# A two-block transformer step on one core: products with tokens on the partitions

## The chip, the cores and the metric

The kernel runs on one core of a Trainium2 chip. A core has a matrix engine (TensorE, "PE" in the profile, with its weight loads as "PEld"), VectorE ("DVE"), ScalarE ("ACT"), GpSimd ("POOL") and SyncE ("SP"), 16 DMA engines, an on-chip memory of 128 partitions (SBUF) and the accumulator banks that PE writes (PSUM). The metric is the device time of one execution, in microseconds (us); lower is better.

## The reference

A sequence of 256 tokens with 1024 features goes through two blocks, all in float32:

```python
def first_block(x, ...):
    h = rms_norm(x, norm1_g)
    y_a = rwkv(h @ w_in[...])             # 8 heads, recurrence with decay
    y_b = sparse_attention(h @ w_in[...]) # 8 heads, top-k keys by an indexer
    ga, gb = sigmoid(h @ w_in[...gates])
    x = x + (ga * (y_a @ w_o_rwkv) + gb * (y_b @ w_o_att)) @ w_out
    h = rms_norm(x, norm2_g)
    x = x + (silu(h @ w_gate) * (h @ w_up)) @ w_ffn_out   # 2816 hidden
    return rms_norm(x, normf_g)

def second_block(x, c, ...):
    sh1, sc1, gt1, sh2, sc2, gt2 = split(silu(c) @ w_ada + b_ada, 6)
    h = rms(x, g_mix) * (1 + sc1) + sh1
    y_a = gated_deltanet(h @ w_in[...])   # conv, chunked delta rule
    y_b = dilated_mixture(h @ w_in[...])  # three window/dilation patterns
    merged = sigmoid(gate_a) * (y_a @ w_up_gdn) + sigmoid(gate_b) * (y_b @ w_up_dil)
    x = x + gt1 * (merged @ w_out)
    h2 = rms(x, g_ffn) * (1 + sc2) + sh2
    return x + gt2 * moe_ffn(h2, ...)     # 64 experts, 8 per token, and a shared one
```

## The kernel before

**How a product is made.** The weights are float32 in DRAM. `wsplit` cuts what a load brought into pieces of 1024 columns and each piece into two matmul-ready parts: ACT casts the high part (`wh`, L269), DVE subtracts it from the weight and writes the rest (`wl`, L270), 512 columns at a time, in a ring of three pieces. Activations are split in the same way (`uh`, `ul`). A product of two such pairs is three matmuls (`mm3`: high by high, high by low, low by high) in the fp32r format.

**How a product lies.** The residual stream `xT` and nearly every activation are feature-major: features on the 128 partitions, the 256 tokens along the free axis, eight blocks side by side. `dense` (L296) holds a 128x128 block of the weights still in PE and moves the 256 tokens past it, so that one PSUM bank takes two blocks of 128 output features. PSUM banks of the tag `d` come in a ring of four. Only the attention values of the two blocks (`vps`, `vdp`) hold the tokens still and move the weights, 256 columns at a time.

**Norms.** `Rms` squares a block (ACT L368), gathers the squares on DVE (L376 to L379) and sums over the partitions by matmuls with ones on PE (`nps`, L386 to L395 turn the sum into 1/rms in each partition). Gains are numbers for a partition.

**The order of work.** Block 1: norm, `w_in` products, RWKV and sparse attention with gate products slipped between their steps (`fill`), then output products: `merge` (L878) multiplies the gate of the attention branch by its output product (DVE L873), adds the other branch (POOL L881), and splits the result into `mgh` (ACT L883) and `mgl` (DVE L884) for the product with `w_out`; the residual sum (DVE L910) and its norm follow. The feed-forward network runs 11 groups of 256 hidden features: the gate and up products of group g+1 stand ahead of the down product of group g, which adds up in four PSUM banks (`acc`, tags `a` and `b`); `gated` (L923) makes the activation between them. During these groups DVE also computes block 2's modulation vector (`ada_step`, 24 steps). Block 2 has the same form: norm and modulation, products, DeltaNet and dilated attention with fills, four rounds of gate product and `merge`, `w_out_2`, norm, router. Then come the experts: 27 half-units that stream 1 MB expert weights, gather the tokens of an expert, run it and scatter its output into four `acc` banks (L1662) by a matmul with a permutation. At the end eight DVE steps (L1759) add `acc` times gt2 to the residual, with an output DMA behind each second step.

PE's instructions run in the order in which the scheduler and, in the expert stage, the code wrote them; an engine that waits holds back all that stands behind it in its own queue.

Of the kernel before, what the change touches and what calls it, by code (L numbers as in the profile page):

```python
# [16 lines left out]
D = 1024  # L17
S = 256
# [118 lines left out]

def lay_out(inp):
# [24 lines left out]
    A["w_in_2"] = wgroups(np.concatenate([w2[:, :4096], w2[:, 4112:]], 1), 256)  # L163
    A["w_ba"] = wgroups(w2[:, 4096:4112], 16)[0]
    A["up_g"] = wgroups(np.asarray(inp["w_up_gdn_2"])[0], 256)
    A["up_d"] = wgroups(np.asarray(inp["w_up_dil_2"])[0], 256)
    A["w_out_2"] = wgroups(np.asarray(inp["w_out_2"])[0], 256)
# [26 lines left out]
def _body(es, tc, A, pat, cat, taps, upto):  # L194
# [111 lines left out]

    def whole(steps):
# [90 lines left out]
    nrm = cp.tile([128, 1], F32, name="nrm")  # L398

# [357 lines left out]
    def dsa_proj():  # L757
# [15 lines left out]
        for i in range(2):  # L773
            rope((yield from dense(A["w_in"][13 + i], uu)), [(every, qi[:, 2 * i:2 * i + 2])])
# [4 lines left out]
        for i in range(2):  # L779
            p = pt("d", "vps")  # L780
            for k, (wh, wl) in enumerate(wblocks(A["w_in"][11 + i], 256)):
                for n in range(2):
                    tk = slice(128 * n, 128 * (n + 1))
                    mm3(p[:, 256 * n:256 * (n + 1)], (uu[0][:, k, tk], uu[1][:, k, tk]), (wh, wl), k == 0 and n == 0, k == NB - 1)
                yield
            nc.scalar.copy(vt[:, :, 256 * i:256 * (i + 1)], p.rearrange("p (n c) -> p n c", n=2))

    ga = ap_.tile([128, NB, S], F32, name="ga", tag="s1", bufs=1)
    gcol = lambda t, g: fl(t[:, 2 * g:2 * g + 2])

    def gate_steps(t, src):

        nc.scalar.activation(t, (yield from dense(src, uu)), AF.Tanh, scale=0.5)
# [5 lines left out]
    for g in range(4):  # L799
        fill.add("ga", gate_steps(gcol(ga, g), A["w_in"][15 + g]))  # L800
# [61 lines left out]
    gb = rp.tile([128, NB, S], F32, name="gb", tag="zr", bufs=2)  # L862
# [25 lines left out]
    for g in range(4):  # L888
        first_term(gcol(ga, g), A["wo_r"][g], ysp, 4)
    for g in range(4):  # L890
        gate_group(gcol(gb, g), g, A["w_in"][19 + g])
    tap("ya", fl(yA))
    tap("yb", fl(yB))
    if upto == 2:
        return
# [3 lines left out]
    for g in range(4):  # L899
        merge(mg, g, gcol(ga, g), gcol(gb, g), A["wo_a"][g], ysp, 4)  # L900
    xT = ap_.tile([128, NB, S], F32, name="hT1", tag="s0", bufs=1)
    norm = Rms(xT, r2(0))
    more_slots(dp, 1, "qq")
    for g in range(4):
# [9 lines left out]
    tap("h1", fl(xT))  # L914
    if upto == 3:
        return
# [6 lines left out]
    def gated(fp, pg, pu, hi, lo):  # L923

        t = fp.tile([128, 512], F32, name="silu", tag="silu")
        nc.scalar.activation(t, pg, AF.Silu)
        nc.vector.tensor_tensor(t, t, pu, op=ALU.mult)
        nc.scalar.copy(hi, t)
        nc.vector.tensor_sub(lo, t, hi.bitcast(F32))

    def accumulate(acc, src, act, first, last):

        order = [(k, ct) for k in range(2) for ct in range(NB)]
        w = iter(wsplit(src))
        if last:
            w, order = list(w), [(k, ct) for ct in range(NB) for k in range(2)]
        parts_ = []
        for k, ct in order:
            if len(parts_) <= k:
                parts_ = list(w) if last else parts_ + [next(w)]  # L940
            wh, wl = parts_[k]
            c = slice(128 * ct, 128 * (ct + 1))
            o = 256 * (ct % 2)
            mm3(acc[ct // 2][:, o:o + 256], (wh[:, c], wl[:, c]), (act[0][:, k, :], act[1][:, k, :]),
                first and k == 0 and ct % 2 == 0, last and k == 1)
# [28 lines left out]
    _, uu, _ = scaled_parts(xT, lambda b: pcol("norm2_g", b), norm.finish())  # L974
    acc = [pt("ab"[i % 2], "acc%d" % i) for i in range(4)]
    steps = iter(range(24))
    gate = lambda g: dense_pair(A["ffn_in"][g], uu)
    acts = []
    pg = gate(0)
    for g in range(11):  # L980
        pu = gate(11 + g)
        acts.append(tuple(fp.tile([128, 2, S], F32R, name="act" + x, bufs=3) for x in "hl"))
        gated(fp, pg, pu, *(fl(x) for x in acts[g]))
        if g < 10:
            pg = gate(g + 1)
# [12 lines left out]
    more_slots(None, 0)
    fx.close()
# [10 lines left out]
    with tc.issue_after(d.ins):  # L1010
        rs1 = norm.finish()
# [802 lines left out]
```

## Time and profile before

| what | us |
|---|---|
| runs of the kernel (three) | 1529.07, 1529.05, 1523.01; median 1529.05 |
| the profiled execution, its own time | 1525.53 |
| its span in the trace | 1523.7 |
| PE busy | 1444.0 |
| DVE busy | 823.8 |
| ACT busy | 586.4 |
| POOL busy | 119.6 |

The span is the time from the first to the last instruction that the profiler saw; about 1.8 us of the execution lie around it. The busy times of the engines overlap. PE's mean granted clock is 0.981 of full speed. The expert stage begins near 1023 us in this trace and lasts for the rest of the span.

### The profile page before, as it was taken

What the parts mean: (1) busy time and instruction counts of PE and PEld (TensorE: products, weight loads), DVE (VectorE), ACT (ScalarE), POOL (GpSimd) and SP (SyncE); (2) the same over time, 40 slices, a digit from 0 to 9 for tenths busy, and PEclk for the clock granted to TensorE, in tenths of its full rate; (3) what the DMA queues carried; (4) which work ended last, traced back from release to release, by engine and by line L of the source; (5) the groups of instructions that cost most, each with busy time, mean ns of one, the idle gap of its engine ahead of it and who ended that gap; (6) DMA issues with size and microseconds to landing.
All of it is one profiled execution on the core that took longest, in us unless ns stands there. A gap on an engine that the chain in (4) does not pass through costs nothing.

```text
span 1523.7 us, 27838 instructions
## 1 busy us (share of the span) xinstructions
PE 1444.0 (95%) x11234; PEld 1162.8 (76%) x11234; DVE 823.8 (54%) x1671; ACT 586.4 (38%) x1200; POOL 119.6 (8%) x120
## 2 busy tenths in 40 slices
PE   6999999989999979899999999989999999989996
PEld 6799998979999969798898999987554544444543
DVE  5787488668888787855855567654122111111211
ACT  5543256545444467444534555442111111111110
POOL 2143210100000000310230000100000000000000
PEclk9999999989999989999999999999999999999999
DMA  6302154649877255222321433983999999999996
GB/s 222 116 31 69 39 172 131 217 177 419 351 290 283 95 191 194 84 83 74 121 84 56 166 115 107 337 325 142 358 405 421 422 421 421 421 422 421 421 421 259
DMA packets 58626, 362.09 MB, mean 238 GB/s; under 512 B 6912, under 2 KB 7552, under 8 KB 20352
## 3 DMA queue, kind: packets, MB, share of 16 engines
q1 hardware_dynamic: 56912, 357.77, 60.6%
q10 hardware_dynamic: 1584, 2.52, 0.5%
q8 instruction: 89, 1.46, 0.4%
q14 instruction: 41, 0.34, 0.1%
HBM read 357.51 MB, written 1.05 MB: 235 GB/s over the span
## 4 chain that ended last, share of the span: by engine, by line
PE 77%; DMA 13%; DVE 6%; ACT 2%; POOL 1%; issue 1%; SPq 0%; DVEq 0%; ACTq 0%; POOLq 0%
PE dps L283 35%; DMA wx<-in_w_exp_dram 9%; PE gup L283 8%; PE acc L283 6%; PE sps L283 5%; PE dnp L283 4%; DMA wh<-in_w_exp_dram 2%; PE gat L283 2%; PE vdp L283 2%; DVE wl L270 1%; PE sps L286 1%; PE sgu L283 1%; DMA wl<-in_w_exp_dram 1%; PE ksp L283 1%; PE vps L283 1%
## 5 line engine op out<-in xcount | busy, mean ns | idle before, releaser
L283 PE MATMUL dps<-uh,wh 128*128 128x256 f32 x1280 | 379.2, 297 | 13.2 <-ACT uh L416 8.9
L283 PE MATMUL dps<-uh,wl 128*128 128x256 f32 x1280 | 369.1, 289 | 2.4 <-DVE wl L270 2.4
L283 PE MATMUL dps<-ul,wh 128*128 128x256 f32 x1280 | 369.6, 289 | 0.1
L283 PEld LDWEIGHTS dps<-uh,wh 128*128 128x128 f32 x1280 | 248.3, 194 | 24.9 <-ACT uh L416 10.3
L283 PEld LDWEIGHTS dps<-ul,wh 128*128 128x128 f32 x1280 | 248.6, 194 | 6.1 <-issue 4.3
L283 PEld LDWEIGHTS dps<-uh,wl 128*128 128x128 f32 x1280 | 248.3, 194 | 4.3 <-DVE wl L270 2.8
L270 DVE TENSOR_TENSOR wl<-w,wh 128x512 fp32r<-128x512 f32 x267 | 193.1, 744 | 68.6 <-ACT wh L269 66.7
L283 PE MATMUL gup<-wx,xg 128*32 128x512 f32 (+2 forms) x1016 | 202.1, 600 | 18.7 <-DMA wx<-in_w_exp_dram 18.6
L269 ACT CAST wh<-w 128x512 fp32r<-128x512 f32 x267 | 154.2, 614 | 147.1 <-PE dps L283 99.9
L269 ACT CAST wh<-wm 128x512 fp32r<-128x512 f32 x200 | 115.7, 618 | 128.5 <-PE dps L283 84.1
L270 DVE TENSOR_TENSOR wl<-wm,wh 128x512 fp32r<-128x512 f32 x200 | 137.7, 718 | 48.8 <-ACT wh L269 48.4
L283 PEld LDWEIGHTS gup<-wx,xg 128*32 128x32 f32 (+2 forms) x1016 | 59.6, 121 | 134.9 <-issue 95.9
L1658 DVE TENSOR_TENSOR yl<-dnp,yh 128x512 fp32r<-128x512 f32 x54 | 37.3, 691 | 156.6 <-ACT yh L1657 156.6
L1632 DVE COPY cs<-pxt 128x1 f32<-128x1 f32 x27 | 4.3, 158 | 213.8 <-PE pxt L286 213.8
L283 PE MATMUL dnp<-wx,hT 128*32 128x512 f32 (+1 forms) x528 | 102.0, 597 | 3.3 <-DMA wx<-in_w_exp_dram 2.5
L1638 ACT ACTIVATE sgx<-gup 128x256 f32<-128x256 f32 x27 | 10.3, 383 | 219.9 <-PE gup L283 219.9
L1657 ACT CAST yh<-dnp 128x512 fp32r<-128x512 f32 x54 | 31.6, 585 | 123.0 <-PE dnp L283 123.0
L283 PEld LDWEIGHTS dnp<-wx,hT 128*32 128x32 f32 (+1 forms) x528 | 27.8, 120 | 48.7 <-issue 39.5
L283 PE MATMUL acc<-PT,yh 128*128 128x256 f32 x216 | 55.2, 293 | 0.0
L283 PE MATMUL gat<-P,hth 128*128 128x256 f32 (+1 forms) x224 | 54.7, 287 | 0.0
L283 PE MATMUL acc<-PT,yl 128*128 128x256 f32 x216 | 53.1, 283 | 0.6 <-DVE yl L1658 0.6
L957 DVE SCALAR_TENSOR_TENSOR ada<-wm,ct,ada 128x512 f32<-128x512 f32 x76 | 53.2, 744 | 0.0
(520 smaller groups left out, 2789.6 us busy)
## 6 DMA issues: line engine op xcount, KB each, us to landing
wx<-in_w_exp_dram SPq DMA_DIRECT2D x159, 1024.0 KB, 16.0
w<-in_w_in_dram SPq DMA_DIRECT2D x44, 1024.0 KB, 4.9
wm<-in_w_ada_dram SPq DMA_DIRECT2D x22, 1024.0 KB, 8.0
wm<-in_w_in_dram SPq DMA_DIRECT2D x21, 1024.0 KB, 4.9
wh<-in_w_exp_dram SPq DMA_DIRECT2D x33, 512.0 KB, 15.9
wl<-in_w_exp_dram SPq DMA_DIRECT2D x33, 512.0 KB, 14.7
wm<-in_ffn_in_dram SPq DMA_DIRECT2D x16, 1024.0 KB, 9.1
wm<-in_ffn_out_dram SPq DMA_DIRECT2D x7, 1024.0 KB, 7.1
```

What stands on the lines that cost most here:

```text
L269: nc.scalar.copy(hi[:, c:e], x[:, c:e])
L270: nc.vector.tensor_sub(lo[:, c:e], x[:, c:e], hi[:, c:e].bitcast(F32))
L283: latest[0] = nc.tensor.matmul(*args, **kw)
L286: latest[0] = nc.tensor.transpose(*args, **kw)
L957: nc.vector.scalar_tensor_tensor(y, x, ct[:, k:k + 1], y, op0=ALU.mult, op1=ALU.add)
L1632: nc.vector.tensor_copy(self.cs, px[:, 256:257])
L1638: nc.scalar.activation(sg, self.pg[:, 0:256], AF.Silu)
L1657: nc.scalar.copy(yh[:, quar(c, 512)], pd)
L1658: nc.vector.tensor_tensor(yl[:, quar(c, 512)], pd, yh[:, quar(c, 512)].bitcast(F32), op=ALU.subtract)
```

## The change

**Products.** `dense_t` replaces `dense` for the values, all gates, all output projections (`wo_r`, `wo_a`, `w_out`, `up_g`, `up_d`, `w_out_2`) and the feed-forward network: a 128x128 block of the activations (128 tokens) stands still in PE and the weights move past it 512 columns wide. It fills two PSUM banks, one for each half of the tokens (n), with 512 output features (c) each; k runs outside, n inside. The products for RWKV's and DeltaNet's inputs, queries, keys and the indexer stay as they were. Weights are laid out for this in DRAM; each load is still 1 MB.

**The residual stream** `xt` is token-major: tokens on the partitions, features along the free axis. `Means` sums the squares along the free axis with ACT's accumulator. Where a product needs the features on the partitions again, `turned` makes four 128x128 PE transposes into a PSUM bank: in `merge`, after both norms of block 1 and block 2's, and twice two transposes in each feed-forward group (`gated`). The vectors gt1 and gt2 are spread over the partitions by eight matmuls each (`gtp`), and the final norm's gain comes as a DRAM array of 128 equal rows (`gfrow`). The scatter holds the permutation still and moves the expert's output 512 wide. At the end DVE multiplies by gt2, and the sum with the residual is DVE's for the first half of the tokens and POOL's for the second.

```diff
+    def dense_t(srcs, u, name="dpt", early=False):
+
+        p = [pt("d", name) for _ in range(2)]
+        srcs = [srcs[i] for i in range(srcs.shape[0])]
+        last = 4 * len(srcs) - 1
+        for i, src in enumerate(srcs):
+            pieces = wsplit(wload(src))
+            for ks in ([range(4)] if early and i == len(srcs) - 1 else [(k,) for k in range(4)]):
+                for n in range(2):
+                    for k4 in ks:
+                        k, o = 4 * i + k4, slice(512 * (k4 % 2), 512 * (k4 % 2) + 512)
+                        wh, wl = pieces[k4 // 2]
+                        mm3(p[n], (u[0][:, k, toks[n]], u[1][:, k, toks[n]]), (wh[:, o], wl[:, o]), k == 0, k == last)
+                        yield
+        return p
+
+    def turned(src, name="trp"):
+
+        p = pt("d", name)
+        for b in range(4):
+            tr(p[:, 128 * b:128 * (b + 1)], src[:, 128 * b:128 * (b + 1)], ident)
+        return p.rearrange("p (b t) -> p b t", b=4)
...
-    def merge(mg, g, t, m, w, y, nk):
-
-        first_term(m, w, y, nk)
-        nc.gpsimd.tensor_tensor(t, t, m, op=ALU.add)
-        hi, lo = (fl(q[:, 2 * g:2 * g + 2]) for q in mg)
-        nc.scalar.activation(hi, t, AF.Copy, scale=0.5)
-        nc.vector.scalar_tensor_tensor(lo, t, 0.5, hi.bitcast(F32), op0=ALU.mult, op1=ALU.subtract)
+    def merge(mg, c, t, m, mc, src, y):
+
+        first_term(m, mc, src, y)
+        for n in range(2):
+            x = t[:, n, c5[c]]
+            nc.gpsimd.tensor_tensor(x, x, m[:, n, c5[mc]], op=ALU.add)
+            p = turned(x)
+            hi, lo = (q[:, 4 * c:4 * c + 4, toks[n]] for q in mg)
+            nc.scalar.activation(hi, p, AF.Copy, scale=0.5)
+            nc.vector.scalar_tensor_tensor(lo, p, 0.5, hi.bitcast(F32), op0=ALU.mult, op1=ALU.subtract)
...
-    for g in range(4):
-        t = r2(1)("xres")
-        nc.scalar.dma_start(out=fl(t), in_=A["xT"][:, 512 * g:512 * (g + 1)])
-        p = dense_pair(A["w_out"][g], mg)
-        if g:
-            norm.pair(g - 1)
-        nc.vector.tensor_tensor(fl(xT[:, 2 * g:2 * g + 2]), p, fl(t), op=ALU.add)
-    norm.pair(3)
+    nc.scalar.activation(nrm, epsd[:, 0:1], AF.Sqrt)
+    for c in range(2):
+        p = whole(dense_t(A["w_out"][c], mg, early=c == 1))
+        for n in range(2):
+            t = fl(r2(1)("xres"))
+            nc.scalar.dma_start(out=t, in_=A["x"][:, D * n + 512 * c:D * n + 512 * (c + 1)])
+            nc.vector.tensor_tensor(xt[:, n, c5[c]], p[n], t, op=ALU.add)
+            means.add(n, 0, c, xt[:, n, c5[c]], nx[:, n, c5[c]])
+    uu = parts()
+
+    def normed2(b, p):
+        g = pcol("norm2_g", b)
+        nc.scalar.activation(uu[0][:, b, toks[n]], p, AF.Copy, scale=g)
+        nc.vector.scalar_tensor_tensor(uu[1][:, b, toks[n]], p, g, uu[0][:, b, toks[n]].bitcast(F32), op0=ALU.mult, op1=ALU.subtract)
+
+    for n in range(2):
+        rs = means.inverse(n)
+        for c in range(2):
+            nc.vector.tensor_scalar(nx[:, n, c5[c]], xt[:, n, c5[c]], rs, None, op0=ALU.mult)
+            p = turned(nx[:, n, c5[c]])
+            for b in range(4):
+                normed2(4 * c + b, p[:, b])
...
+    def gated(p, hi, lo):
+
+        q = pt("d", "act").rearrange("p (b t) -> p b t", b=2)
+        for n in range(2):
+            t = fp.tile([128, 256], F32, name="silu", tag="silu")
+            nc.scalar.activation(t, p[n][:, 0:256], AF.Silu)
+            nc.vector.tensor_tensor(t, t, p[n][:, 256:512], op=ALU.mult)
+            for b in range(2):
+                tr(q[:, b, toks[n]], t[:, 128 * b:128 * (b + 1)], ident)
+        nc.scalar.copy(hi, q)
+        nc.vector.tensor_sub(lo, q, hi.bitcast(F32))
...
+    means = Means(2)
+    for n in range(2):
+        for c in range(2):
+            x, y = xt[:, n, c5[c]], hg[:, n, c5[c]]
+            nc.vector.tensor_tensor(x, acc[n][c], x, op=ALU.add)
+            nc.vector.tensor_tensor(y, x, gfrow[:, c5[c]], op=ALU.mult)
+            for kind, z in enumerate((x, y)):
+                j = fp.tile([128, 512], F32, name="junk", tag="junk", bufs=2)
+                means.add(n, kind, c, z, j)
+        rsb = means.inverse_both(n)
+        for c in range(2):
+            q = fp.tile([128, 512], F32, name="hq", tag="hq", bufs=2)
+            nc.vector.tensor_scalar(q, hg[:, n, c5[c]], rsb, None, op0=ALU.mult)
+            p = turned(q)
+            for b4 in range(4):
+                b = 4 * c + b4
+                hi, lo = (z[:, b, toks[n]] for z in uu)
+                t = fp.tile([128, 128], F32, name="ht", tag="ht", bufs=4)
+                nc.scalar.activation(hi, p[:, b4], AF.Identity, scale=cf[:, b:b + 1], bias=md[:, b:b + 1])
+                nc.vector.tensor_scalar(t, p[:, b4], cf[:, b:b + 1], md[:, b:b + 1], op0=ALU.mult, op1=ALU.add)
+                nc.vector.tensor_sub(lo, t, hi.bitcast(F32))
+    for n in range(2):
+        rs1 = means.inverse(n)
+        nc.gpsimd.tensor_scalar(xt[:, n], hg[:, n], rs1, None, op0=ALU.mult)
...
+    gt1 = tp.tile([128, D], F32, name="gt1")
+    for c in range(2):
+        p = pt("d", "gtp")
+        for b in range(4):
+            mm(p[:, 128 * b:128 * (b + 1)], md[:, 16 + 4 * c + b:17 + 4 * c + b].to_broadcast([128, 128]), ident, start=True, stop=True)
+        nc.scalar.copy(gt1[:, c5[c]], p)
...
-    for g in range(4):
-        t = fl(tmp("sgm"))
-        gate_group(t, g, A["w_in_2"][38 + g])
-        merge(mg, g, gcol(ga, g), t, A["up_d"][g], (yB2[:, 0], yB2[:, 1]), 4)
-        prefetch(1)
-    norm = Rms(xT, tmp)
-    for g in range(4):
-        p = dense_pair(A["w_out_2"][g], mg)
-        prefetch(1)
-        if g:
-            norm.pair(g - 1)
-        for i in range(2):
-            b = 2 * g + i
-            nc.vector.scalar_tensor_tensor(xT[:, b, :], p[:, 256 * i:256 * (i + 1)], md[:, 16 + b:17 + b], xT[:, b, :], op0=ALU.mult, op1=ALU.add)
-    norm.pair(3)
+    for c in range(2):
+        t = tmp("sgm")
+        gate_group(t, 0, A["w_in_2t"][5 + c])
+        merge(mg, c, ga, t, 0, A["up_d"][c], (yB2[:, 0], yB2[:, 1]))
+        prefetch(2)
+    nx = ap_.tile([128, 2, D], F32, name="nx2", tag="s1", bufs=1)
+    means = Means()
+    nc.scalar.activation(nrm, epsd[:, 0:1], AF.Sqrt)
+    for c in range(2):
+        p = whole(dense_t(A["w_out_2"][c], mg, early=c == 1))
+        prefetch(2)
+        for n in range(2):
+            x, y = xt[:, n, c5[c]], nx[:, n, c5[c]]
+            nc.vector.tensor_tensor(y, p[n], gt1[:, c5[c]], op=ALU.mult)
+            nc.vector.tensor_tensor(x, x, y, op=ALU.add)
+            means.add(n, 0, c, x, y)
...
-            for b in range(NB):
-                for j, part in enumerate(self.y):
-                    mm(acc[b // 2][:, quar(b % 2, 256)], part[:, quar(b, 128)], self.PT, start=False,
-                                     stop=last and j == 1, skip_group_check=True)
+            for c in range(2):
+                for n in range(2):
+                    for j, part in enumerate(self.y):
+                        mm(acc[n][c], self.PT[:, toks[n]], part[:, c5[c]], start=False, stop=last and j == 1, skip_group_check=True)
...
-    for b in range(NB):
-        nc.vector.scalar_tensor_tensor(xT[:, b, :], acc[b // 2][:, quar(b % 2, 256)], md[:, 40 + b:41 + b], xT[:, b, :], op0=ALU.mult, op1=ALU.add)
-        if b % 2:
-            c = slice(256 * (b - 1), 256 * (b + 1))
-            nc.sync.dma_start(out=A["out"][:, c], in_=fl(xT)[:, c])
+    gt2 = mp.tile([128, D], F32, name="gt2", tag="xg", bufs=2)
+    for c in range(2):
+        p = pt("d", "gtp")
+        for b in range(4):
+            mm(p[:, 128 * b:128 * (b + 1)], md[:, 40 + 4 * c + b:41 + 4 * c + b].to_broadcast([128, 128]), ident, start=True, stop=True)
+        nc.scalar.copy(gt2[:, c5[c]], p)
+    for c in range(2):
+        for n in range(2):
+            x = xt[:, n, c5[c]]
+            t = mp.tile([128, 512], F32, name="fin", tag="P", bufs=2)
+            nc.vector.tensor_tensor(t, acc[n][c], gt2[:, c5[c]], op=ALU.mult)
+            (nc.gpsimd if n else nc.vector).tensor_tensor(x, x, t, op=ALU.add)
+            nc.sync.dma_start(out=A["out"][:, D * n + 512 * c:D * n + 512 * (c + 1)], in_=x)
```

Three places, as the instructions stand in each engine's queue. First PE's queue in block 1, at the end of the last attention output product (`yBs` is the attention output) and the start of the `w_out` product (`mgh`, `mgl`). Before:

```order
L283 MATMUL dps<-yBs,wh 128x256 x2
L283 MATMUL dps<-yBs,wl 128x256
L283 MATMUL dps<-yBs,wh 128x256 x2
L283 MATMUL dps<-yBs,wl 128x256
L283 MATMUL dps<-mgh,wh 128x256
L283 MATMUL dps<-mgl,wh 128x256
L283 MATMUL dps<-mgh,wl 128x256
L283 MATMUL dps<-mgh,wh 128x256
```

and with the change (`trp` are the transposes of the merged sum `ga`):

```order
L295 MATMUL dpt<-wl,yBs 128x512
L295 MATMUL dpt<-wh,yBs 128x512 x2
L295 MATMUL dpt<-wl,yBs 128x512
L295 MATMUL dpt<-wh,yBs 128x512
L298 MATMUL trp<-cst_74,ga 128x128 x8
L295 MATMUL dpt<-wh,mgh 128x512
L295 MATMUL dpt<-wl,mgh 128x512
L295 MATMUL dpt<-wh,mgl 128x512
```

The eight transposes now stand between the two products, and the same eight stand between the first and the second half of the attention output product.

Second, DVE's queue over the same merges; `gb` is L873's product of gate and projection, `mgl` the split of the merged sum, `wl` the split of weights. Before:

```order
L873 SCALAR_TENSOR_TENSOR gb<-gb,dps 128x512
L270 TENSOR_TENSOR wl<-w,wh 128x512 x2
L884 SCALAR_TENSOR_TENSOR mgl<-ga,mgh 128x512
L873 SCALAR_TENSOR_TENSOR gb<-gb,dps 128x512
L884 SCALAR_TENSOR_TENSOR mgl<-ga,mgh 128x512
L270 TENSOR_TENSOR wl<-w,wh 128x512
L873 SCALAR_TENSOR_TENSOR gb<-gb,dps 128x512
L270 TENSOR_TENSOR wl<-w,wh 128x512 x3
L884 SCALAR_TENSOR_TENSOR mgl<-ga,mgh 128x512
```

with the change:

```order
L282 TENSOR_TENSOR wl<-w,wh 128x512 x12
L935 SCALAR_TENSOR_TENSOR gb<-gb,dpt 128x512 x2
L282 TENSOR_TENSOR wl<-w,wh 128x512 x2
L949 SCALAR_TENSOR_TENSOR mgl<-trp,mgh 128x4x128 x2
L282 TENSOR_TENSOR wl<-w,wh 128x512 x2
L935 SCALAR_TENSOR_TENSOR gb<-gb,dpt 128x512 x2
L282 TENSOR_TENSOR wl<-w,wh 128x512 x2
L949 SCALAR_TENSOR_TENSOR mgl<-trp,mgh 128x4x128 x2
L282 TENSOR_TENSOR wl<-w,wh 128x512 x2
```

The split of the merged sum now reads the transposes' bank (`trp`) and comes in two pairs, each behind a pair of `gb`.

Third, PE's queue between the feed-forward network and block 2, from its last down product (`acc`) to the first product of block 2 (`dps`). Before:

```order
L283 MATMUL acc_3764<-actl,wh 128x256
L283 MATMUL acc_3764<-acth,wl 128x256
L283 MATMUL nps<-nsg,ones 128x256
L283 MATMUL nps<-nsq,ones 128x256
L283 MATMUL nps<-nsg,ones 128x256
L283 MATMUL nps<-nsq,ones 128x256
L283 MATMUL nps<-nsg,ones 128x256
L283 MATMUL nps<-nsq,ones 128x256
L283 MATMUL nps<-nsg,ones 128x256
L283 MATMUL nps<-nsq,ones 128x256
L283 MATMUL dps<-uh,wh 16x256
L283 MATMUL dps<-uh,wh 128x256
```

with the change (`hq` is the normalised residual):

```order
L295 MATMUL acc_3371<-wh,acth 128x512
L295 MATMUL acc_3371<-wl,acth 128x512
L295 MATMUL acc_3371<-wh,actl 128x512
L298 MATMUL trp<-cst_74,hq 128x128 x16
L295 MATMUL dps<-uh,wh 16x256
L295 MATMUL dps<-uh,wh 128x256
L295 MATMUL dps<-ul,wh 16x256
L295 MATMUL dps<-uh,wl 16x256
```

The eight sums over the partitions (`nps`) are gone, and sixteen transposes stand there.

## Rows read from the trace of the kernel before

**Rows 1.** The page's busy times: engine, us, share of the span, instructions.

```profile
PE 1444.0 (95%) x11234; PEld 1162.8 (76%) x11234; DVE 823.8 (54%) x1671; ACT 586.4 (38%) x1200; POOL 119.6 (8%) x120
```

**Rows 2.** Windows: length; busy us of PE, PEld, DVE, ACT, POOL; clock, DMA share, GB/s.

```profile
346.00:526.00 180.00, 178.59 (x1486) 175.54 (x1485) 150.19 (x244) 83.42 (x148) 0.00 (x0) 1.00 0.75 295
958.30:1004.80 46.50, 46.50 (x388) 46.45 (x388) 30.77 (x43) 23.83 (x43) 6.61 (x4) 1.00 0.93 359
1052.00:1260.00 208.00, 206.59 (x1538) 110.43 (x1534) 39.31 (x102) 35.20 (x77) 0.00 (x0) 1.00 0.99 401
555.00:958.00 403.00, 393.12 (x3125) 364.89 (x3125) 267.94 (x543) 206.01 (x426) 44.33 (x40) 0.98 0.32 108
```

**Rows 3.** Chain that ended last: start, us, instructions of one piece.

```profile
202.36 11.53 PE vps L283 x96
958.30 46.07 PE dps L283 x384
```

**Rows 4.** Timeline of PE at the start, at half clock: start, us.

```profile
21.23 0.41 PE L283 MATMUL dps<-uh,wh 128*128 128x256 f32 x1
...
22.51 0.41 PE L283 MATMUL dps<-uh,wh 128*128 128x256 f32 x1
```

**Rows 5.** Timeline of PE in the expert stage: 512-column f32, then 128-column fp32r.

```profile
1116.49 3.70 PE L283 MATMUL gup<-wx,xg 128*128 128x512 f32 x8
...
1123.56 0.41 PE L283 MATMUL pxt<-pcp,P 128*64 128x1 f32 x8
...
1474.20 0.27 PE L283 MATMUL gat<-P,htl 128*128 128x128 f32 x1
...
1475.76 0.27 PE L283 MATMUL gat<-P,htl 128*128 128x128 f32 x1
```

**Rows 6.** Chain, four transposes in one piece.

```profile
526.87 0.44 PE adt L286 x4
```

**Rows 7.** Groups by line and shape on DVE, POOL and ACT: busy us, mean ns.

```profile
L873 DVE SCALAR_TENSOR_TENSOR gb<-gb,dps 128x512 f32<-128x512 f32 x4 | 2.7, 681 | 0.4 <-PE dps L283 0.4
L881 POOL TENSOR_TENSOR ga<-ga,sgm 128x512 f32<-128x512 f32 x4 | 6.6, 1652 | 196.0 <-DVE sgm L873 196.0
L718 DVE TENSOR_SCALAR yAB<-zps,par 128x128 f32<-128x128 f32 x8 | 2.9, 403 | 7.3 <-PE zps L286 7.3
L1336 DVE TENSOR_TENSOR yB<-pvd,yB 128x128 fp32r<-128x128 f32 x8 | 2.3, 289 | 3.8 <-ACT yB L1335 3.8
L368 ACT ACTIVATE nsq<-hT 128x512 f32<-128x512 f32 x16 | 9.8, 625 | 13.6 <-DVE hT L1436 8.3 <-DVE hT L910 2.6 <-DVE hT L996 1.9
L839 ACT ACTIVATION_READ_ACCUMULATOR lx<-lx,st 128x1 f32 x16 | 3.0, 186 | 0.0
L371 ACT ACT_TABLE_LOAD x4 | 5.1, 1283 | 0.1
```

**Rows 8.** Chain behind the first merges and at two seams.

```profile
310.06 8.60 PE dps L283 x59
...
337.94 7.69 PE dps L283 x40
...
1019.55 3.75 DMA wr<-in_w_rt_dram
```

**Rows 9.** Windows of three seams and of a stretch behind the router.

```profile
305.00:312.00 7.00, 4.80 (x29) 4.14 (x28) 6.07 (x9) 2.90 (x6) 1.65 (x1) 0.82 0.43 150
331.00:338.00 7.00, 1.74 (x6) 0.61 (x4) 5.91 (x11) 2.65 (x6) 0.00 (x0) 0.67 0.63 220
537.30:547.50 10.20, 4.19 (x18) 2.63 (x16) 9.13 (x20) 4.74 (x11) 0.35 (x1) 0.88 0.44 155
1025.50:1035.70 10.20, 10.20 (x43) 9.35 (x43) 4.52 (x39) 3.42 (x5) 0.65 (x2) 0.63 0.44 183
```

**Rows 10.** Timeline of DVE and SP at the end of the program.

```profile
1515.77 2.83 DVE L1759 SCALAR_TENSOR_TENSOR hT<-acc,md,hT 128x256 f32<-128x256 f32 x7
...
1516.27 2.68 SPq L1762 DMA_DIRECT2D out_dram<-hT  x4
```

More of the change, by code (lines that the diff above doesn't have):

```diff
@@ L778, in dsa_proj, with gate_steps @@
             rope((yield from dense(A["w_in"][9 + i], uu)), [(hf, kz[hf, 2 * i:2 * i + 2, a, :]) for a, hf in enumerate(halves)])
-        for i in range(2):
[L780 to L793, printed above, removed]
+        p = yield from dense_t(A["w_in_t"][0], uu, "vps")
+        for n in range(2):
+            nc.scalar.copy(vt[:, n, :], p[n])
+    ga = ap_.tile([128, 2, D], F32, name="ga", tag="s1", bufs=1)
+    def gate_steps(t, c, src):
+        p = yield from dense_t(src, uu)
+        for n in range(2):
+            nc.scalar.activation(t[:, n, c5[c]], p[n], AF.Tanh, scale=0.5)
     for g in range(2):
@@ L859, in _body @@
             attend(n, j)
[L862 removed]
+    gb = rp.tile([128, 2, D], F32, name="gb", tag="zr", bufs=2)
     def split_y(y, t):
@@ L921, in _body @@
     more_slots(fp, 9)
[L923 to L929, printed above, removed]
+    gfrow = fp.tile([128, D], F32, name="gfrow", bufs=1)
+    nc.scalar.dma_start(out=gfrow, in_=A["gfrow"])
+    def gated(p, hi, lo):
[8 more added lines that the diff above has]
+        nc.vector.tensor_sub(lo, q, hi.bitcast(F32))
     def accumulate(acc, src, act, first, last):
-        order = [(k, ct) for k in range(2) for ct in range(NB)]
-        w = iter(wsplit(src))
+        w = wsplit(wload(src))
+        order = [(k, n, c) for k in range(2) for n in range(2) for c in range(2)]
         if last:
[L936 to L945, printed above, removed]
+            order = [(k, n, c) for n in range(2) for c in range(2) for k in range(2)]
+        for k, n, c in order:
+            mm3(acc[n][c], (act[0][:, k, toks[n]], act[1][:, k, toks[n]]), tuple(x[:, c5[c]] for x in w[k]),
+                first and k == 0, last and k == 1)
     md = ap_.tile([128, 48], F32, name="md")
@@ L1353, in _body, with project_v @@
     dil = [Dilated(i) for i in range(2)]
-    ga = ap_.tile([128, NB, S], F32, name="ga2", tag="s1", bufs=1)
+    ga = ap_.tile([128, 2, D], F32, name="ga2", tag="s1", bufs=1)
+    vd = gp.tile([128, 2, 3, 512], F32, name="vd")
+    def project_v():
+        for gi in range(3):
+            p = yield from dense_t(A["w_in_2t"][gi], uu, "vdp")
+            for n in range(2):
+                nc.scalar.copy(vd[:, n, gi, :], p[n])
     for hp in range(2):
@@ L1358, in _body @@
         fill.add("qkv", gdn_proj(hp))
-    for d in dil:
-        fill.add("v", d.project_v())
-    for g in range(4):
-        fill.add("gates", gate_steps(gcol(ga, g), A["w_in_2"][34 + g]))
+    fill.add("v", project_v())
+    for c in range(2):
+        fill.add("gates", gate_steps(ga, c, A["w_in_2t"][3 + c]))
     fill.among(gdn(0), gdn(1))
@@ L1367, in _body @@
     fill.add("dil1", dil[1].project())
-    for g in range(4):
-        fill.add("first", first_steps(gcol(ga, g), A["up_g"][g], (yA2[:, 0], yA2[:, 1]), 8))
+    for c in range(2):
+        fill.add("first", first_steps(ga, c, A["up_g"][c], (yA2[:, 0], yA2[:, 1])))
     fill.finish("v")
@@ L1474, in shared_down @@
         for f in range(2):
-            for b in range(NB):
-                mm(acc[b // 2][:, 256 * (b % 2):256 * (b % 2 + 1)], wsh[2][f][:, 128 * b:128 * (b + 1)], hsh[:, f, :],
-                   start=f == 0 and b % 2 == 0, stop=False, skip_group_check=True)
+            for n in range(2):
+                for c in range(2):
+                    mm(acc[n][c], hsh[:, f, toks[n]], wsh[2][f][:, c5[c]], start=f == 0, stop=False, skip_group_check=True)
         release(wsh[2:])
```

196 lines of the change are left out of this document (99 added, 97 removed).

## The prediction

> **What bounds the kernel now.** I read the busy times first. PE is busy for 95% of the span, DVE for 54% [rows 1]. A mean over stages hides their limits, so the windows came next [rows 2]. In the feed-forward stretch PE is busy 178.6 of 180 us, DVE 150.2; over DeltaNet and dilated attention 393.1 of 403; in the gates and merges before block 2's output 46.5 of 46.5. PE is the bound of all of them, and a nanosecond off a matmul there is a nanosecond off the end. In the expert stretch PE looks just as busy, but the DMA share is 0.99 at 401 GB/s: there the weights' transfer sets the pace. So a cheaper scatter is worth nothing, and whatever the earlier stages save or lose moves the expert stage as a whole, one to one.
>
> The chain gives the price of a matmul in those stages: 46.07 us for 384 and 11.53 for 96, so 120 ns for 256 columns [rows 3]. The second of these is `vps`, which holds tokens and moves weights already: which operand moves doesn't change the price. The timeline at half clock shows what part of it is the stream: six steps in 1.28 us, 213 ns each for 256 columns, hence 106.7 ns at full clock [rows 4]. About 13 ns per matmul are not the stream.
>
> Last I read the seams, where PE waits: the end of block 1's merges, and the steps from one layer to the next [rows 8, 9].
>
> **The gain: 512 columns in one matmul.** Two matmuls of 256 cost 240 ns; one of 512 isn't in the trace in fp32r. It can't be below 2 x 106.7 = 213 ns, and nothing suggests more than 240. Nearest are the experts' f32 matmuls with 512 columns: 16 records in 7.07 us, 442 ns each, 2 x 221 [rows 5], and the weight load doesn't lengthen it, since 128-column matmuls, each with a load of its own, follow each other at 111 ns (14 steps in 1.56 us) [rows 5]. I take 220: 20 ns saved for each pair.
>
> The Trainium skill, "TensorE: Matmul & The Clock Gate", section "Back-to-back issue gap", gives N/2.4 + 2.5 ns for a warm matmul of N columns: 109 for 256, where this trace has 120, and 216 for 512. By it the pair would save 24 instead of 20, and the sum below would come out near 1522. The same section has 131 ns for N = 512 in a sustained stream of load and matmul; by that the kernel would fall under 1400, and I give it 1 in 100, since no row here has PE stream a column faster than 213 ns for 512.
>
> Pairs before the experts, counted from the code (256-wide matmuls, by two): block 1's values, gates and output products 432; feed-forward 11 groups x 72 = 792; block 2's fills (values, first gates, `up_g`) 336; the second gates, `up_d` and `w_out_2` 240. That is 1800, or 36.0 us. Not all of it arrives: 144 pairs are filled in between the attention's steps in block 1, where PE partly waits for others (I count half), and of the 336 fills a third, since that stretch leaves PE 10 us idle in any case [rows 2]. That takes off 1.4 and 2.2: **gain 32.4 us**.
>
> **What is added on PE.** A 128x128 transpose takes 0.11 us (0.44 for four) [rows 6]. Each feed-forward group has four: 44 x 0.11 = **4.8**. They stand behind the 24 down matmuls of the group before (5.3 us), which cover silu and product; only the first group has nothing in front of it: **1.0**. The eight `gtp` matmuls ahead of block 2's merges stand in a busy stretch: **0.9**; the other eight are in the tail.
>
> **The merges.** Before, the last product's split was waited for only at the start of `w_out`: PE idled 2.2 us of [rows 9]'s first window (7.00 less 4.80 busy). Now PE has transposes of the merged sum behind each of the four halves, and nothing else to do in its queue. The chain from the last matmul of a half: DVE multiplies both token halves, 0.68 each [rows 7]; the first can start 0.7 early, since its bank closes three matmuls sooner. POOL then adds, 1.65 for each 512-wide half, one after the other [rows 7], and four transposes follow: 0.1 + 2 x 1.65 + 0.44, with hand-overs 4.0 us, of which 0.9 is transposes. Four times 4.0 less the 2.2 that go: **+13.8**. If POOL's adds were free it would be 3.3 us less for each; it has no cover, since PE's queue has no other work there.
>
> **The clock.** After an idle stretch the granted clock drops. Behind the first merges 59 matmuls took 8.60 us instead of 7.08: 1.5 lost after gaps of 2.2. Behind the seam to the feed-forward network 40 took 7.69 instead of 4.80: 2.9 lost [rows 8]. Behind the router the clock is 0.63 for 10.2 us, 3.8 lost [rows 9]. The new waits of 3.1 us lie between the first two: 2.0 each, four times, less the 1.5 there are: **+6.5** (bounds 0 and 3.8 each: -1.5 and +13.7).
>
> **The seams.** From `w_out` to the feed-forward network the norm now needs no matmuls, but adds squares, a transpose and eight ACT and DVE splits of a 128-token tile for each token half, and PE's first k with both halves is the ninth of these. Worked out in the same way it is 7.2 us against the 6.9 now, from 331.0 to the first product at 337.94 [rows 8, 9]: **0**. At the router the start waits for a DMA, 3.75 us [rows 8], and the new norm may be 1.3 faster; I count **0**.
>
> From the feed-forward network to block 2 the wait is 10.2 us now [rows 9]. The new one: ACT squares eight 512-wide tiles (0.625 and 0.186 for reading the sum) and loads a table (1.28) [rows 7]; half lies beside the last down products, since the first token half closes 12 matmuls early, so its 1/rms is there after about 4 us. Then DVE has three scalings of up to 0.68 and nine tiles with two steps each, 0.403 + 0.289, before the second half's first tile is ready [rows 7], and transposes twice 0.44: 4 + 2.0 + 6.2 + 0.9, some 13.1, with hand-overs 13.5. **+3.3** (12 to 14.5).
>
> **The tail.** Before, the last steps of DVE end at 1518.6 and each second one issues its output [rows 10]; about 1.6 us lie between the last scatter and the last step. Now six `gtp` matmuls follow the last scatter (0.7), ACT copies (0.6), DVE has five 512-wide steps at 0.68 ahead of POOL's last add (1.65): 6.35. Less 1.6, and with the output's four transfers spread out more, **+4.0** (3 to 5).
>
> **The sum.** 4.8 + 1.0 + 0.9 + 13.8 + 6.5 + 3.3 + 4.0 = 34.3 us of costs against 32.4: +1.9. On the profiled execution's 1525.5 that is 1527.4. This execution lies 3.5 below the median; the mean of it and the three runs is 1526.7, so I forecast **1529 us**: no change that a measurement can tell. (0.5%, 7.6 us, is about what a measurement of this kernel can tell from none.)
>
> **The rivals.**
> - *Faster: the merges stay warm and the long matmul is near its stream.* For it: the waits of 3.1 us are short, and a matmul of twice the length has one issue instead of two. Against it: 2.2 us of gaps were enough for a loss of 1.5 us. At 215 ns the gain is 32.4 x 25/20 = 40.5; with no clock loss at the merges, costs are 26.3: 14.2 less on 1526.7, about **1513**; either alone gives 1521. Chance 0.28.
> - *Slower: the merges cost the clock as the router does.* 3.8 us four times instead of 2.0: +7.2, **1536**; it decides from about 3.3 a merge on. For it: two waits stand 24 matmuls apart, so the second may come before the clock is back. Chance 0.12.
> - *Slower: the feed-forward network becomes DVE's.* DVE's 150 us in a stretch of 180 stay, PE's fall to 168. DVE runs in order: where silu's product stands behind splits of weights and `ada_step`, the transposes wait in PE's queue, and 1 us for each group would be 11: **1540**. It decides when the product comes more than 5.3 us after the gate. Against it: 84 to 90% is still less than all. Chance 0.12.
> - *Slower: 512 columns cost nearly two 256s.* At 230 half the gain goes: **1545**. Against it only the f32 rows. Chance 0.08.
>
> The forecast keeps 0.40. The low end, 1512, is the first rival; the high end, 1547, is the second and third together. The first leaves 0.28 for faster; the slower rivals, less what of them stays within 0.5%, give 0.30; the rest, 0.42, is no change.
>
> **What the changed profile would show.** Records of `dpt` at a pitch of 220 ns (right), at 213 to 216 or above 227 (wrong). Four waits of PE in front of `trp`, each released by POOL, some 3 us long, with a clock near half behind them. A feed-forward group of 16.3 us with PE busy above 98%; gaps in front of the transposes there would show the third rival. A start of block 2's products 13 to 14 us after the last down product. A last output issue some 6 us after the last scatter. The forecast is wrong if the merges don't stall, or if a stage that I took as covered (weights' splits on DVE) becomes the bound.

## The result, and the profile after

The changed kernel takes 1548.64 us (median of four runs, 1547.76 to 1549.44) against 1526.74 before: a ratio of 1.0146, 95% interval 1.0119 to 1.0172. It is slower by 22 us, where 1529 and no change were forecast, and just above the range's end of 1547.

The page's busy times and windows of the changed kernel (columns as in [rows 1, 2]); the windows are the feed-forward stretch, the two merges of block 1, the seam up to block 2's first product, the 59 us behind it, and block 2's gates and merges:

```profile
PE 1443.6 (93%) x9326; PEld 1059.8 (69%) x9326; DVE 824.0 (53%) x1695; ACT 600.1 (39%) x1253; POOL 128.0 (8%) x124
```

```profile
346.00:526.00 180.00, 177.47 (x808) 142.16 (x807) 151.94 (x256) 84.21 (x157) 0.00 (x0) 1.00 0.74 289
...
286.30:305.30 19.00, 14.11 (x66) 10.81 (x64) 13.98 (x17) 8.21 (x15) 5.89 (x4) 0.97 0.47 167
...
534.30:545.90 11.60, 3.16 (x18) 2.35 (x17) 10.25 (x28) 8.86 (x23) 5.67 (x2) 0.72 0.07 28
545.90:605.00 59.10, 46.83 (x343) 44.63 (x342) 36.47 (x86) 33.90 (x66) 0.31 (x1) 0.82 0.47 170
968.40:1012.30 43.90, 38.91 (x178) 31.43 (x177) 23.02 (x31) 19.10 (x34) 5.89 (x4) 0.96 0.81 320
```

PE's busy time is what it was, 1444 us: a sixth fewer matmuls, many of them longer. Its share of the span fell. To see where, I cut both traces at the same points of the program, by the starts of PE's records:

| stretch | before, us | after | difference |
|---|---|---|---|
| start to the attention's values | 202.2 | 200.3 | -1.9 |
| values, attention, first gates | 45.3 | 42.8 | -2.5 |
| first output product, second gates | 43.8 | 43.2 | -0.6 |
| merges of block 1 | 11.3 | 19.0 | +7.6 |
| `w_out`, seam | 35.3 | 31.4 | -3.9 |
| feed-forward network | 199.3 | 197.5 | -1.8 |
| seam to block 2's first product | 10.3 | 11.8 | +1.4 |
| block 2 up to the end of dilated attention | 410.5 | 422.5 | +12.0 |
| gates and merges of block 2 | 34.6 | 44.0 | +9.3 |
| `w_out_2`, seam to the router | 30.8 | 29.4 | -1.4 |
| experts | 493.3 | 492.2 | -1.1 |
| tail | 7.0 | 12.1 | +5.1 |

Three things stand out. The stretches that got mostly wider matmuls gained little: the feed-forward network 1.8 us where the forecast has 15.8 less 5.8. Both merges lost time, as forecast. And block 2 lost 12 us behind its first product, in a place where I had looked for a small gain.

**The wide matmul.** The timeline of PE in the changed kernel, ten down products in a row (start, us):

```profile
449.78 0.40 PE L295 MATMUL acc<-wh,acth 128*128 128x512 f32 x1
...
451.88 0.39 PE L295 MATMUL acc<-wh,acth 128*128 128x512 f32 x1
```

Nine steps in 2.10 us: 233 ns. Over the trace's steady stretches the products of block 1's normed activations step by 227, the down products by 233 in the mean (single steps up to 236), `w_out_2`'s by 233, and no product has a mean near 220.

**Behind the seam.** In 59.1 us after block 2's first product PE issues 343 matmuls; the kernel before issues 448 in the same time:

```profile
547.50:606.60 59.10, 57.35 (x448) 53.95 (x449) 47.07 (x100) 41.28 (x79) 0.00 (x0) 0.93 0.53 190
```

The changed kernel's timeline of PE, of SP (which issues the loads) and of DVE shows the reason; in brackets, the idle time before and what ended it:

```profile
534.12 0.39 PE L295 MATMUL acc<-wh,actl 128*128 128x512 f32 x1
...
545.89 0.56 PE L295 MATMUL dps<-uh,wh 128*16 128x256 f32 x1
549.47 0.58 PE L295 MATMUL dps<-uh,wh 128*128 128x256 f32 x1 [3.01 <-DVE ht L1093]
...
564.74 1.86 PE L295 MATMUL gps<-gl,cst 128*128 128x16 f32 x8 [4.08 <-DVE gl L1128]
571.62 0.58 PE L295 MATMUL dps<-uh,wh 128*128 128x256 f32 x1 [5.02 <-ACT wh L281]
...
645.30 0.60 PE L298 MATMUL sps<-cst,nm 128*128 128x128 f32 x4
```

```profile
528.12 19.19 SPq L268 DMA_DIRECT2D w<-in_w_in_dram  x3
556.09 0.33 SPq L224 DMA_DIRECT2D cst<-in_consts_dram  x1
556.45 23.08 SPq L268 DMA_DIRECT2D wm<-in_w_in_dram  x4
```

```profile
555.71 0.29 DVE L1094 TENSOR_TENSOR ul<-ht,uh 128x128 fp32r<-128x128 f32 x1
```

The loads of block 2's constants and of its next weights go out at 556.1, right behind the last of the split tiles at 556.0, and 22 us after the last down product. In the kernel before, SP issues the same two 6.3 us after it:

```profile
543.50 0.37 SPq L212 DMA_DIRECT2D cst<-in_consts_dram  x1
543.92 26.85 SPq L256 DMA_DIRECT2D wm<-in_w_in_dram  x4
```

Block 2's slots for weights lie where the feed-forward network's pool was (`fp`), and the change put the norm's temporaries (`hq`, `ht`, `junk`) into this pool: it can't be given up before the last tile is split. PE waits 5.0 us for weights, having waited 4.1 us for a gate vector, and the clock is at 0.82 over the 59 us. At the first product of block 2's recurrence (`sps`) the kernel lies 15.4 us behind where it lay, both counted from the last down product: 111.2 us behind it, where the kernel before had 95.8:

```profile
537.22 0.28 PE L283 MATMUL acc<-acth,wl 128*128 128x256 f32 x1
...
633.04 0.60 PE L286 MATMUL sps<-cst,nm 128*128 128x128 f32 x4
```

**A merge**, the two waits in front of its second half's transposes, and POOL's two adds for that half:

```profile
302.82 0.66 PE L298 MATMUL trp<-cst,ga 128*128 128x128 f32 x4 [1.44 <-POOL ga L945]
304.49 1.12 PE L298 MATMUL trp<-cst,ga 128*128 128x128 f32 x4 [1.02 <-POOL ga L945]
```

```profile
301.49 2.95 POOL L945 TENSOR_TENSOR ga<-ga,gb 128x512 f32<-128x512 f32 x2 [6.40 <-DVE gb L935]
```

And the clock behind each of the four pairs of waits, first and second half of block 1, then of block 2 (the clock is the third number from the end):

```profile
295.20:298.60 3.40, 3.40 (x17) 2.88 (x18) 1.74 (x3) 0.60 (x1) 0.00 (x0) 1.00 0.05 22
304.10:307.40 3.30, 2.91 (x9) 2.52 (x10) 2.18 (x3) 0.61 (x2) 0.34 (x1) 0.50 0.21 82
990.20:993.50 3.30, 3.30 (x11) 2.71 (x11) 1.60 (x3) 0.60 (x1) 0.00 (x0) 0.50 1.02 425
1012.00:1015.40 3.40, 3.40 (x17) 2.84 (x18) 1.70 (x3) 0.60 (x1) 0.00 (x0) 1.00 1.00 424
```

### The profile page after: what moved, and what is told of

It reads as the page before. It is cut to its first block, busy times and chain, and to the rows that moved or that the text cites. A ratio compares the mean times of both kernels' runs of the same rounds, so it can differ in the third digit from the quotient of the medians.

```text
span 1546.0 us, 24067 instructions
## 1 busy us (share of the span) xinstructions
PE 1443.6 (93%) x9326; PEld 1059.8 (69%) x9326; DVE 824.0 (53%) x1695; ACT 600.1 (39%) x1253; POOL 128.0 (8%) x124
## 5 line engine op out<-in xcount | busy, mean ns | idle before, releaser
L295 PE MATMUL gup<-wx,xg 128*32 128x512 f32 (+2 forms) x1016 | 202.2, 604 | 19.2 <-DMA wx<-in_w_exp_dram 19.2
L295 PE MATMUL dps<-uh,wh 128*128 128x256 f32 (+1 forms) x672 | 202.0, 301 | 11.8 <-ACT wh L281 5.0
L295 PE MATMUL dps<-uh,wl 128*128 128x256 f32 x672 | 195.1, 291 | 2.4 <-DVE wl L282 2.4
L295 PE MATMUL dps<-ul,wh 128*128 128x256 f32 x672 | 195.5, 292 | 0.2
L295 PEld LDWEIGHTS dps<-uh,wh 128*128 128x128 f32 (+1 forms) x672 | 130.5, 194 | 20.0 <-issue 6.3
L295 PEld LDWEIGHTS dps<-ul,wh 128*128 128x128 f32 x672 | 130.2, 194 | 5.8 <-issue 4.4
L295 PEld LDWEIGHTS dps<-uh,wl 128*128 128x128 f32 x672 | 130.4, 194 | 4.1 <-DVE wl L282 2.9
L295 PE MATMUL dpt<-wh,uh 128*128 128x512 f32 x304 | 124.8, 411 | 1.6 <-DVE ul L979 1.6
L295 PE MATMUL dpt<-wh,ul 128*128 128x512 f32 x304 | 120.6, 397 | 0.0
L295 PE MATMUL dpt<-wl,uh 128*128 128x512 f32 x304 | 120.4, 396 | 0.0
L295 PEld LDWEIGHTS dpt<-wh,uh 128*128 128x128 f32 x304 | 58.1, 191 | 15.0 <-issue 2.3
```

What stands on the lines that cost most here:

```text
L295: latest[0] = nc.tensor.matmul(*args, **kw)
```

## The experiments

The theory (A in most expectations): four losses that don't depend on each other, namely a wide matmul that saves about 10 ns a pair and not 20; loads held back by a pool; waits for POOL at the merges; a longer tail. Each has its rival in its expectation. Runs of the kernel before beside them are at 1525 to 1528.

**e1: no temporaries in the feed-forward pool.** The residual `x` is dead once it is squared, and takes their place:

```diff
-                j = fp.tile([128, 512], F32, name="junk", tag="junk", bufs=2)
-                means.add(n, kind, c, z, j)
+                means.add(n, kind, c, z, x)
...
-            q = fp.tile([128, 512], F32, name="hq", tag="hq", bufs=2)
+            q = xt[:, n, c5[c]]
...
-                t = fp.tile([128, 128], F32, name="ht", tag="ht", bufs=4)
+                t = q[:, 128 * b4:128 * (b4 + 1)]
```

> The temporaries of the norm ahead of block 2 (hq, ht, junk) lie in the residual's own tile instead of the feed-forward network's memory pool, so that this pool can be given up, and block 2's first weights can be loaded into its place, before the 16 tiles are split. Theory A (the loads wait for the pool: in the changed kernel they were issued 22 us after the last down product instead of 6): they go out about 3 us after it, the lag that block 2 gained at its start (15.4 us at its first recurrence) falls to 4 or less, and the kernel runs at about 1536. Theory B (the splitting of the tiles by turns on ACT and DVE, 0.94 us each, is what delays block 2): the loads go out early, but the lag stays above 10 and the time within 3 us of 1548.6.

1534.19 us, ratio to before 1.0045 (1.0029 to 1.0061): 14.4 us returned. SP's timeline, the window behind block 2's first product, and PE's last down product and first `sps`:

```profile
538.48 0.33 SPq L224 DMA_DIRECT2D cst<-in_consts_dram  x1
538.85 0.90 SPq L268 DMA_DIRECT2D wm<-in_w_in_dram  x2
```

```profile
551.10:610.00 58.90, 58.35 (x472) 55.53 (x471) 43.64 (x92) 42.91 (x83) 3.43 (x2) 0.96 0.46 162
```

```profile
536.55 0.39 PE L295 MATMUL acc<-wh,actl 128*128 128x512 f32 x1
...
633.75 0.60 PE L298 MATMUL sps<-cst,nm 128*128 128x128 f32 x4
```

The loads go out 1.9 us after the last down product, PE is busy for 58.4 of 58.9 us, and the lag at the recurrence falls from 15.4 to 1.4 us (97.2 less 95.8): 14.0 of the 14.4 us. The tiles are still split by turns, and the first product starts even later (14.6 us after the last down product, not 11.8). Theory A.

**e2: two matmuls of 256 for each of 512**, all else as changed:

```diff
-            mm3(acc[n][c], (act[0][:, k, toks[n]], act[1][:, k, toks[n]]), tuple(x[:, c5[c]] for x in w[k]),
-                first and k == 0, last and k == 1)
+            for j in range(2):
+                q = slice(512 * c + 256 * j, 512 * c + 256 * j + 256)
+                mm3(acc[n][c][:, 256 * j:256 * j + 256], (act[0][:, k, toks[n]], act[1][:, k, toks[n]]), tuple(x[:, q] for x in w[k]),
+                    first and k == 0 and j == 0, last and k == 1)
```

(and the same in `dense_t`).

> As the changed kernel, but each 512-wide matmul of dense_t and of the down products is two of 256 columns; all else the same. Theory A (a fixed 13 ns for each fp32r matmul beside its stream, and a few ns more in some places; pitch 227 to 236 against 2 x 120): the feed-forward stretch gets about 792 x 9 = 7 us longer, the kernel 14 to 16 us: 1563. Theory B (the wide matmul bought nothing, the stretches are paced by the weights' splits): no change within 3 us.

1566.0 us (1563.24 to 1566.97): 17.4 more than the changed kernel. Its timeline:

```profile
449.79 0.28 PE L295 MATMUL dpt<-wh,uh 128*128 128x256 f32 x1
...
450.87 0.28 PE L295 MATMUL dpt<-wh,uh 128*128 128x256 f32 x1
```

Nine steps in 1.08 us, 120 ns, as in [rows 3]. So the width by itself gives 17.4 us, 9.7 ns for each of 1800 pairs, and not 32.4. Theory A, with a little more than it said.

**e3: the transposes later in PE's queue.** The first half's stand behind the other half's attention product (block 1) or gate product (block 2), the second half's behind 24 matmuls of `w_out`:

```diff
-    for c in range(2):
-        merge(mg, c, ga, gb, c, A["wo_a"][c], ysp)
+    add_up(0, ga, gb, 0, A["wo_a"][0], ysp)
+    add_up(1, ga, gb, 1, A["wo_a"][1], ysp)
+    turn(mg, 0, ga)
...
-        p = whole(dense_t(A["w_out"][c], mg, early=c == 1))
+        p = whole(dense_t(A["w_out"][c], mg, early=True)) if c else part_way(A["w_out"][c], 8, lambda: turn(mg, 1, ga))
```

(`add_up` is `merge` up to POOL's sum, `turn` the rest, `part_way` steps a product and calls `turn` between.)

> The transposes of each merged half stand later in PE's queue: behind the other half's attention product in block 1, behind the next gate product in block 2, and for the second half behind the first 24 matmuls of w_out and of w_out_2. Theory A (PE idles 2.4 us in front of each of the four, and the clock then costs 1.7): the four waits go, 1548.6 less 10 to 14, about 1537. Theory B (the wait only moves on, to the splits mgh and mgl or to weights whose splits are queued behind them): less than 4 us.

1536.27 us, ratio 1.0059 (1.0040 to 1.0078): 12.4 us less than the changed kernel. PE's timeline at the first place:

```profile
297.68 1.03 PE L298 MATMUL trp<-cst,ga 128*128 128x128 f32 x8
299.05 0.50 PE L295 MATMUL dpt<-wh,mgh 128*128 128x512 f32 x1 [0.33 <-ACT mgh L952]
```

No wait in front of the transposes, 0.33 us behind them, and no stretch of half clock at the merges of either block:

```profile
297.70:308.00 10.30, 9.46 (x47) 7.14 (x46) 7.20 (x12) 5.36 (x10) 2.99 (x2) 1.00 0.49 177
991.30:1006.00 14.70, 14.37 (x71) 11.60 (x70) 11.13 (x16) 8.21 (x16) 3.02 (x2) 1.00 0.89 361
```

Theory A.

**e4: gt2 early**, one half-unit before the end, and DVE for the last sum:

```diff
-            (nc.gpsimd if n else nc.vector).tensor_tensor(x, x, t, op=ALU.add)
+            (nc.gpsimd if n > c else nc.vector).tensor_tensor(x, x, t, op=ALU.add)
```

> gt2 is spread over the partitions one half-unit before the end instead of behind the last scatter, and the last quarter's sum is DVE's instead of POOL's. Theory A (the tail's chain is gtp, copy, DVE, POOL): the last output is issued about 3 us after the last scatter instead of 7, 1548.6 less 4. Theory B (the end is the output's own transfer): less than 1 us.

1545.22 us, 3.4 less than the changed kernel, by medians of four runs whose spreads nearly touch. The trace bears it out: from the last scatter's start to the span's end are 7.9 us instead of 12.1. Theory A; in DVE's queue one multiplication still waits 0.84 us for POOL.

**e5: the three together.**

> The three edits together: no temporaries in the feed-forward pool, the transposes later, gt2 early. Theory A (three independent losses: 14.4, 12.3 and 3.4 us by themselves): 1548.6 - 30 = 1518 to 1520, 0.4 to 0.6% faster than the kernel before. Theory B (the losses share a cover, as the stall at block 2's start does with the clock): above 1525, no gain over the kernel before.

1518.85 us, ratio to before 0.9961 (0.9947 to 0.9974). By themselves the three returned 14.4, 12.4 and 3.4 us, 30.2 in sum; together 29.8. They don't share a cover: theory A.

**e6: a bank at a time.** In e5 the first product of block 2 comes 14.6 us after the last down product, against 10.3 before. I thought that ACT and DVE held each other up at the tiles of one bank.

```diff
-                nc.scalar.activation(hi, p[:, b4], AF.Identity, scale=cf[:, b:b + 1], bias=md[:, b:b + 1])
-                nc.vector.tensor_scalar(t, p[:, b4], cf[:, b:b + 1], md[:, b:b + 1], op0=ALU.mult, op1=ALU.add)
+            nc.vector.tensor_tensor(t, p, g, op=ALU.mult)
+            nc.vector.tensor_tensor(t, t, sh, op=ALU.add)
+            nc.scalar.copy(hi, t)
```

> As the three mended together, and the norm ahead of block 2 is split a bank at a time: DVE alone reads the transposes (product with the gain and sum with the shift, 512 wide), ACT casts the high part from the result and DVE subtracts. Theory A (ACT and DVE take turns at the tiles of one bank, 0.94 us for each of 16): the first product of block 2 starts 3 to 5 us earlier and the time falls by 2 to 5 us against the three mended. Theory B (the turns are hidden behind the table load and the square roots): within 1 us of them.

1522.27 us, 3.4 more than e5, and the first product 15.5 us after the last down product. The theory falls. In this trace DVE gets to the second half's sum of squares (L458, at 537.91) only behind the first half's steps, which gave the next theory.

**e9 and e8: both halves' 1/rms first**, without and with the padding of e7:

```diff
-        rsb = means.inverse_both(n)
+    rsbs = [means.inverse_both(n) for n in range(2)]
+    for n in range(2):
+        rsb = rsbs[n]
```

> The same without the padding. Theory A: 2 to 3 us under the three mended, about 1516, and the aligned kernel 2.4 us under this one. Theory B: as the three mended, 1519.

> The three mended together, and both halves' 1/rms ahead of block 2 are worked out before either half is split, and the padding of the aligned kernel. Theory A (in DVE's queue the second half's sums of squares stand behind the first half's splits, and the first product of block 2 needs both halves): it starts 2 to 3 us earlier after the last down product than the 14.6 us of the three mended; with 2.4 us from the aligned tiles the kernel runs at 1514, 0.7% faster than the kernel before. Theory B (the start is bound by the splits themselves): only the 2.4 us, 1516 to 1517.

e9: 1520.17 us, as e5; the first product comes 15.0 us after the last down product. That theory falls too. By the traces the late start is not dear: at the product with the gate vector (`gps`) e5 lies only 1.1 us and e9 1.3 us behind the kernel before, counted from the last down product. In e8's seam DVE is busy for 14.55 of 16.5 us and ACT for 12.53:

```profile
528.00:544.50 16.50, 5.61 (x24) 4.14 (x24) 14.55 (x49) 12.53 (x33) 3.16 (x2) 0.57 0.60 237
```

DVE is busy for 88% of it and ACT for 76%, so little seems left for another order to give back; that is argued and not shown, and taking work off DVE was not tried. e8 itself takes 1517.74 us, ratio to before 0.9941 (0.9927 to 0.9955), 2.4 less than e9: the lowest median of all, though its interval overlaps that of e5.

**e7: aligned tiles**, on the changed kernel, a single run:

```diff
+    pad = fp.tile([128, 112], F32, name="pad", bufs=1)
...
+    pad = tp.tile([128, 112], F32, name="pad")
```

> As the changed kernel, with 448 bytes of padding ahead of the activations of the feed-forward network and of the merged sum of block 2, so that these tiles, which stand still in PE, start at multiples of 512 bytes in their partitions, as block 1's normed activations do. Theory A (the stationary tile's place sets whether a 512-wide matmul takes 227 or 231 to 236 ns): the down products fall to 227 and w_out_2's from 233 to 227, 264 x 7 + 96 x 6 = 2.4 us in all. Theory B (the kind of accumulator bank or the order of the products sets it): 231 to 236 as before.

Its timeline in the down products:

```profile
450.37 0.39 PE L295 MATMUL acc<-wh,acth 128*128 128x512 f32 x1
...
452.86 0.39 PE L295 MATMUL acc<-wh,actl 128*128 128x512 f32 x1
```

Eleven steps in 2.49 us, 226 ns, where the changed kernel had 233; `w_out_2`'s fell from 233 to 227. The same 772 matmuls of the feed-forward network take 1.7 us less (e7, then the changed kernel):

```profile
364.00:533.80 169.80, 168.37 (x772) 136.00 (x771) 143.55 (x243) 80.00 (x154) 0.00 (x0) 1.00 0.70 274
```

```profile
362.60:534.10 171.50, 170.07 (x772) 136.11 (x771) 144.09 (x243) 80.15 (x154) 0.00 (x0) 1.00 0.70 273
```

One run at 1548.86 can't show 2.4 us; e8 against e9 bears it out by medians of six and four runs, whose spreads just touch (1519.41 and 1519.24).

## Why the prediction was wrong

**What bounds the kernel** was read rightly: PE up to the experts, DMA there. The experts' stretch moved as a whole (493.3 and 492.2 us).

**"I take 220: 20 ns saved for each pair"** is the term that was mis-sized most. At best the wide matmul takes 227: 213 of stream and 13 to 14 that aren't, the same 13 that [rows 3, 4] gave for 256 columns. The nearest row was in the same kernel and format, and I passed it over for the f32 one [rows 5]. With the placement of tiles (e7) it was 9.7 ns in the mean, by e2: 17.4 us of gain instead of 32.4. The Trainium skill, "TensorE: Matmul & The Clock Gate", section "Back-to-back issue gap", with 216 ns for 512 columns, is farther off still; the measured step decides. That was the rival "512 columns cost nearly two 256s", with a chance of 0.08, and half the gain did go.

**The seam to block 2 (+3.3)** failed in its reach. The first product came 11.8 us after the last down product, earlier than the 13.5 I had worked out, but PE then waited 3.0 us more for split tiles, so that 11.8 against 13.5 says little for the term. And I stopped at the first product. I counted what ACT, DVE and PE do there and never asked SP's queue: which loads are next, and what frees their place. The loss of 15.4 us at the first recurrence is 12 us more than the term, and e1 returned 14.4 by moving three temporaries: with the loads early, the seam's own loss is 1.4 us by then.

**The merges (13.8) and the clock (6.5)** were right in mechanism and too dear in size. Each half waits 2.46 us and not 3.1, in good part since POOL's two adds take 2.95 us and not 3.30. Each block's two halves see one stretch of half clock of 3.4 us, 1.7 us lost, not two of 2.0 each; why the other pair of waits, as long, left the clock alone stays open. e3 returned 12.4 us; with the 32 transposes that stay (32 x 0.11 = 3.5) the merges cost some 16, less the old 2.2 and 1.5: about 12 where the forecast has 20.3.

**The tail (+4.0)** cost 5.1, by the chain that was named. **Feed-forward transposes** (4.8 and 1.0): their 44 records stand at 0.11 each in the stretch, with one wait of 1.1 us in front of the first group; DVE didn't become the bound (151.94 of 180 us). In e2, with the steps of before, the feed-forward network takes 205.6 us, 6.3 more than before: these two terms were right, and the width returned 8.1 us there of the 15.8. **The `gtp` matmuls** of block 2 left 16 records and took 1.7 us, 0.8 more than said. **The other seams**: the router's is 7.1 us where it was 7.0, as said; that to the feed-forward network 8.8 instead of 7.2, 1.6 more than said.

Together: 15 us too much gain, 12 us of the seam missed, 1.6, 1.1 and 0.8 in smaller terms, 8 us of merges charged and not paid, 22.5 against a miss of some 20 (1548.6 for a sum that came to 1528.6). None of the rivals for slower would have named the largest new loss.

## What to carry to other kernels

Where an edit puts temporaries into a memory pool, look up what is loaded into that memory next: the loads wait for the pool's last reader, however cheap that is, and the trace shows it as a gap in the DMA issues and not as a wait of the engine that was edited. Price a longer matmul from the same format's shorter one, as its stream and a fixed part, before a neighbour in another format. Where an in-order engine has a step in its queue that waits for a chain through others, the step may be able to stand one product later, as all four halves of the merges did here.

## What the runs showed of the hardware

The place in SBUF of the tile that stands still in PE changes the step of a 512-wide fp32r matmul. In the changed kernel the same kind of product steps by 227 ns in block 1 (`w_out`) and by 233 in block 2 (`w_out_2`): by the built program's addresses block 1's merged sum starts at a multiple of 512 bytes in its partitions, block 2's 64 bytes beyond one. The down products' activations, also 64 bytes beyond one, step by 233, and 448 bytes of padding in front of both brought them to 227 while the moving weights stayed in their place (e7). Which alignment is enough, and whether the load or the read of the moving operand loses the time, was not tried.

All eight waits at the merges of the changed kernel are alike, 1.42 to 1.53 us and then 1.01 to 1.02. Behind two pairs of them the granted clock fell to half (1.2 GHz) for 3.4 us, behind the other two it stayed at 2.4, and in e2, with waits of the same lengths, it stayed at 2.4 behind all four. In e3, where PE waits 0.33 us there, it stayed at 2.4 too.
